# Four of six modulation chunks of layer 0 summed as rows on VectorE instead of on TensorE, no row sums in the first MLP tiles, two order tables replaced

## The chip, the cores and the metric

The kernel runs on one core of a Trainium2 chip. A core has TensorE (PE, matrix products, with its weight loads shown as PEld), VectorE (DVE), ScalarE (ACT), GpSimd (POOL) and SyncE (SP, which issues most DMA transfers). Each engine takes its own instructions in program order; semaphores hold an instruction until what it needs is there. The metric is the device time of one execution in microseconds (us).

## The reference

Two layers work on 512 latent tokens of width 1024 with 256 context tokens beside them. Each layer is modulated by six vectors that come from one conditioning vector, and each has an MLP:

```
mod_l = split(silu(c) @ ada_w[i] + ada_b[i], 6)              # six chunks of 1024 per layer
a = rmsnorm(h, norm1_g[i]) * (1 + mod_l[1]) + mod_l[0]
# layer 0: differential attention (4 heads) || Hyena-2 channels, one input, one output projection
# layer 1: multi-scale pooling mixer
h = h + mod_l[2] * y
h = h + mod_l[5] * (relu((rmsnorm(h, norm2_g[i]) * (1 + mod_l[4]) + mod_l[3]) @ w1[i]) ** 2 @ w2[i])
```

Layer 0 uses chunks 0 and 1 for the context tokens too. Chunk 2 is wanted at the end of layer 0's mixing, chunks 3 and 4 at its MLP's norm, chunk 5 behind the MLP. The output is the final RMS norm of h.

## The kernel before

Matrices of fp32 are split into a high part of 12 bits and a low rest, and a product is three passes: high by high, high by low, low by high. So each weight tile of 128x1024 is loaded by SP into a ring of four buffers (`sraw`), its high part is made on ACT (`whi`) and its low part on POOL or DVE (`wlo`).

The first third (start and mixing of layer 0) follows two tables, `START` and `MIDDLE`: each word is a step and its number, as `u12`, and a last `v` or `g` puts its elementwise work on DVE or POOL. `play` runs the steps in the order of the table, and that is the order on every engine. The steps that matter here:

- `lg`, `gv`, `ga`, `gt`, `gm`: load chunks 1 and 0 of layer 0 from `adaN`, multiply them with silu(c) and silu(c_ctx) on PE (accumulator `gav`, four products side by side with 32 columns of weights each), copy the sums out and transpose them to columns (`gat`), finish the vectors.
- `lr`, `rv`, `ra`, `rt`, `rm`: the same for chunks 2 to 5 by silu(c): 32 loads of 128x1024 into `sraw`, 16 products steps on PE (accumulator `rav`), then copy, transpose, finish.
- `sb`, `sc`: silu(c) spread over all partitions as a row (`sbcl`).
- `hw`: small products that only keep PE at work. `kp`, `ny`: the spectrum of the Hyena filter (`kp`, `kn`).
- `x`, `w`, `r`: load, high part and low part of an input weight tile. `u`: four products of an input projection. `vm`, `va`, `vh`, `vl`: the attention values, product, bias on DVE (which frees one of two accumulators), high and low part. `S`, `M`, `E`, `C`: attention scores, row maxima on DVE, exponentials on ACT, combination.

Behind the tables comes layer 0's output projection and then Python loops: an MLP of four blocks; a block has eight tiles `f` (first matrix, with `f_out`: relu and square on ACT, square again and low part on DVE) and eight tiles `r` (second matrix, `h_add` on DVE); block 0 does its first four `f` in halves, and block 3 ends with the norm of what follows. Layer 1's modulation is summed in these loops by `grow`: each call multiplies a loaded 128x1024 piece of the transposed `ada_w` with `sbcl` on DVE and sums its rows (one `tensor_tensor_reduce`, shown as CUSTOM_DVE_ANT_0 and a read of the accumulator), 48 in all. In block 0 it is called twice a tile `f`, elsewhere once a tile.

```
        for b in range(4):
            pe.matmul(dst[32 * b : 32 * b + 32, :], sil2[:, 2 * k : 2 * k + 32],
                      srcs[b // 2][:, b % 2 * T : (b % 2 + 1) * T], ...)   # gemv_tile, L571
```

Of the kernel before, what the change touches and what calls it, by code (L numbers as in the profile page):

```python
# [12 lines left out]
ALU = mybir.AluOpType  # L13
# [80 lines left out]
def body(ctx: ExitStack, tc: tile.TileContext, I, out):  # L94
# [517 lines left out]
    rav = {}  # L612
# [15 lines left out]
    @step("rm")
    def row_mods(r):
        gr = gat[1 + r][:, 0]  # L630
        o = (2 + 2 * r) * ND
        if r == 0:
            pairs = ((mods[:, 0, 2, :], 0), (mods[:, 0, 3, :], 1))
        else:
            pairs = ((mods[:, 0, 5, :], 1),)
            dst = smul[:, 1, :]
            dve.tensor_tensor(out=by_half(dst), in0=gr[:, 0], in1=by_half(gpre[:, 1, :]), op=ALU.add)
            dve.tensor_tensor(out=dst, in0=dst, in1=pr("n2g", 0, ND), op=ALU.mult)
        for dst, c in pairs:
            dve.tensor_tensor(  # L640
                out=by_half(dst), in0=gr[:, c], in1=by_half(pr("ada_b", o + c * ND, o + (c + 1) * ND)), op=ALU.add
            )
# [1372 lines left out]
```

## Time and profile before

| what | value |
|---|---|
| median of 3 runs (lowest, highest) | 1135.11 us (1133.04, 1138.07) |
| profiled execution, its own time | 1135.81 us |
| its span, first to last instruction | 1134.0 us |
| mean granted TensorE clock | 0.992 |
| PE busy | 1106.3 us, 98% of the span |
| DVE, ACT, POOL busy | 638.0, 440.5, 396.2 us |

The three runs spread by 0.44%. A busy PE is not a PE at its peak, since its instructions overlap: two matmuls of 128x512 behind each other start about 0.23 us apart, and each is shown with about 0.39 us. So the start-to-start distances tell what a product costs. Where the profile gives an idle time in square brackets, it names what ended it.

### The profile page before, as it was taken

Reading aid. Unit: us, or ns where it says so; the run is one execution under the profiler, and the core shown is the slowest. Engines: PE = TensorE matmul, PEld = TensorE weight load, DVE = VectorE, ACT = ScalarE, POOL = GpSimd, SP = SyncE. Lnnn points to the kernel's source line nnn. Section 1 sums busy time; section 2 is a strip of 40 time slices with the busy share of each in tenths; the row PEclk is TensorE's granted clock in tenths of the full one; section 3 lists DMA queues with packets and bytes.
Section 4 is the critical chain, followed back from the end, with each engine's and each line's share of the span. In section 5 each row is a group of like instructions: output and inputs, shape, how many; then the busy total and the mean of one; then the engine's idle time right before and its main releaser. Section 6 shows DMA issues by size and latency. Waiting matters only on the chain.

```text
span 1134.0 us, 14938 instructions
## 1 busy us (share of the span) xinstructions
PE 1106.3 (98%) x5876; PEld 922.4 (81%) x5876; DVE 638.0 (56%) x964; ACT 440.5 (39%) x741; POOL 396.2 (35%) x307
## 2 busy tenths in 40 slices
PE   8999999999999999999999999999999999999996
PEld 6578787888989978888888888899888888888886
DVE  5855237988965686677677532677323322332334
ACT  3563235666743531142232133366322412412331
POOL 4453245766664511122123113355211221131212
PEclk9999999999999999999999999999999999999998
DMA  9777555113642357657567523213232231231302
GB/s 334 282 239 247 169 203 158 48 40 101 204 168 97 108 167 246 217 167 250 198 202 243 184 75 111 75 38 112 76 110 75 87 137 55 94 113 73 112 1 75
DMA packets 48651, 161.38 MB, mean 142 GB/s; under 512 B 5250, under 2 KB 8578, under 8 KB 48452
## 3 DMA queue, kind: packets, MB, share of 16 engines
q1 hardware_dynamic: 46132, 149.93, 39.1%
q0 software_dynamic: 2448, 10.49, 2.7%
q8 instruction: 46, 0.75, 0.3%
q14 instruction: 25, 0.20, 0.1%
HBM read 156.20 MB, written 4.20 MB: 141 GB/s over the span
## 4 chain that ended last, share of the span: by engine, by line
PE 85%; DVE 6%; DMA 3%; ACT 3%; issue 2%; POOL 1%; SPq 0%; POOLq 0%; ACTq 0%; DVEq 0%
PE r L201 11%; PE r L197 11%; PE r L195 11%; PE f L201 9%; PE f L197 9%; PE f L195 9%; PE v L890 3%; PE u L201 2%; PE u L195 2%; PE u L197 2%; DMA g<-in_adaN 2%; PE rav L571 1%; DVE nl L1523 1%; PE wk L408 1%; PE f L1624 1%
## 5 line engine op out<-in xcount | busy, mean ns | idle before, releaser
L164 POOL TENSOR_TENSOR wlo<-raw,whi 128x1024 fp32r<-128x1024 f32 x77 | 194.9, 2534 | 524.8 <-ACT whi L163 381.4
L197 PE MATMUL r<-gl,whi 128*128 128x512 f32 (+1 forms) x576 | 207.3, 368 | 2.1 <-DVE gl L1615 2.1
L163 ACT CAST whi<-raw 128x1024 fp32r<-128x1024 f32 x135 | 140.0, 1043 | 178.3 <-PE r L197 153.4
L195 PE MATMUL r<-gh,whi 128*128 128x512 f32 (+1 forms) x576 | 207.6, 369 | 0.0
L195 PE MATMUL f<-nh,whi 128*128 128x512 f32 (+1 forms) x512 | 191.4, 379 | 0.0
L197 PE MATMUL f<-nl,whi 128*128 128x512 f32 (+1 forms) x512 | 191.3, 378 | 0.0
L1536 DVE SCALAR_TENSOR_TENSOR h<-r,mods,h 128x512 f32<-128x512 f32 (+1 forms) x81 | 54.3, 671 | 170.6 <-PE r L201 170.4
L1614 DVE TENSOR_TENSOR r<-r 128x512 f32<-128x512 f32 (+1 forms) x72 | 53.9, 749 | 165.4 <-ACT gh L1613 165.2
L1612 ACT ACTIVATE r<-f 128x512 f32<-128x512 f32 (+1 forms) x72 | 39.6, 550 | 236.5 <-PE f L201 234.9
L201 PE MATMUL r<-gh,wlo 128*128 128x512 f32 (+1 forms) x576 | 131.4, 371 | 0.0
L197 PEld LDWEIGHTS r<-gl,whi 128*128 128x128 f32 x576 | 108.5, 188 | 21.6 <-DVE gl L1615 2.5
L195 PEld LDWEIGHTS r<-gh,whi 128*128 128x128 f32 x576 | 108.6, 189 | 19.3
L201 PE MATMUL f<-nh,wlo 128*128 128x512 f32 (+1 forms) x512 | 121.3, 379 | 0.0
L201 PEld LDWEIGHTS r<-gh,wlo 128*128 128x128 f32 x576 | 101.2, 190 | 19.1
L195 PEld LDWEIGHTS f<-nh,whi 128*128 128x128 f32 x512 | 96.2, 188 | 19.0
L197 PEld LDWEIGHTS f<-nl,whi 128*128 128x128 f32 x512 | 96.3, 188 | 18.9
L201 PEld LDWEIGHTS f<-nh,wlo 128*128 128x128 f32 x512 | 92.3, 188 | 18.9
L1465 DVE CUSTOM_DVE_ANT_0 g<-g,sbcl 128x1024 f32<-128x1024 f32 x48 | 98.6, 2054 | 0.4 <-DMA g<-in_adaT 0.4
L164 DVE TENSOR_TENSOR wlo<-raw,whi 128x1024 fp32r<-128x1024 f32 x58 | 76.4, 1317 | 8.4 <-ACT whi L163 8.4
L195 PE MATMUL u<-ah,whi 128*128 128x512 f32 x160 | 63.3, 396 | 0.0
L197 PE MATMUL u<-al,whi 128*128 128x512 f32 x160 | 62.6, 391 | 0.0
L1485 ACT ACTIVATE sq<-h 128x256 f32<-128x256 f32 (+1 forms) x47 | 21.4, 460 | 80.4 <-DVE h L1536 80.4
(373 smaller groups left out, 1847.2 us busy)
## 6 DMA issues: line engine op xcount, KB each, us to landing
raw<-in_w SPq DMA_DIRECT2D x128, 512.0 KB, 4.5
g<-in_adaN SPq DMA_DIRECT2D x48, 512.0 KB, 5.6
g<-in_adaT SPq DMA_DIRECT2D x48, 512.0 KB, 3.5
raw<-in_w_hy SPq DMA_DIRECT2D x12, 512.0 KB, 3.9
raw<-in_w_qk SPq DMA_DIRECT2D x8, 512.0 KB, 5.2
pth<-in_pth POOLq DMA_DIRECT2D x4, 768.0 KB, 6.3
raw<-in_w_out SPq DMA_DIRECT2D x5, 512.0 KB, 4.0
x<-in_xT SPq DMA_DIRECT2D x8, 256.0 KB, 5.2
```

What stands on the lines that cost most here:

```text
L163: act.copy(out=hi, in_=src)
L164: (lo_eng or dve).tensor_tensor(out=lo, in0=src, in1=f32(hi), op=ALU.subtract)
L195: pe.matmul(ps, wh[:, c], ah[i][:, t0 : t0 + n], start=(i == 0), stop=False)
L197: pe.matmul(ps, wh[:, c], al[i][:, t0 : t0 + n], start=False, stop=False)
L201: pe.matmul(ps, wl[:, i * P : (i + 1) * P], ah[i][:, t0 : t0 + n], start=False, stop=(i == k - 1))
L408: pe.matmul(t[:, 0:P], idn, idn, start=True, stop=True)
L890: pe.matmul(pp[:, :256], a, b, start=(k == 0 and e == 0), stop=(k == ND - 1 and e == 2))
L1465: dve.tensor_tensor_reduce(out=gin[k], in0=gin[k], in1=sbc[0], scale=1.0, scalar=0.0, op0=ALU.mult, op1=ALU.add, accum_out=mods[:, layer, ...
L1485: act.activation(out=sq, in_=hs[d][:, seg], func=AF.Square)
L1536: dve.scalar_tensor_tensor(out=hs[d][:, seg], in0=pp[:, :n], scalar=gate[:, d : d + 1], in1=hs[d][:, seg], op0=ALU.mult, op1=ALU.add)
L1612: act.activation(out=r, in_=pp[:, :n], func=AF.Relu)
L1614: dve.tensor_tensor(out=r, in0=r, in1=r, op=ALU.mult)
```

## The change

1. Chunks 2 to 5 of layer 0 come from the transposed `ada_w` (which now holds both layers) and are summed as `grow` does it: 32 steps `rv`, each one `tensor_tensor_reduce` on DVE. The 16 product steps, two copies on ACT and eight transposes on PE go; `rm` is now four steps of one or two small additions on DVE. `sb` and `sc` stand ahead of the first `rv`.
2. `grow` is no longer called in block 0's tiles `f`; since 48 sums are wanted, the last eight now fall in block 3's tiles `f`.
3. Both tables hold another order, and other engines for some elementwise steps.

```diff
 START = """
-ws0v lx7 lx0 lx6 hw7 fm0 hw15 lx1 hw11 kc0 wh0 ft0 al0 hw5 gp0 fs0 lx3 sq3 fm1 wl0v ws1v ld0 sq7 hw13 hw0 lx5 lc2 lx2
+ws1v lx0 lg4 hw11 fm0 hw13 ft0 hw22 lx2 hw0 fs0 sq2 gp0 fm1 ws0v hw4 hw23 hw2 hw5 wh1 gp3 ft1 wh0 lx4 lx1 sq1 fs1 wl1v
...
@@ row_load
-        nc.sync.dma_start(out=rows_in[k], in_=I["adaN"][k % 16 // 2, :, 2 + 2 * (k // 16) + k % 2, :])
+        nc.sync.dma_start(out=rows_in[k], in_=I["adaT"][0, (2 * ND + k) * P : (2 * ND + k + 1) * P, :])
@@ row, row_out, row_t, row_mods
-    @step("rv")
-    def row(n):
-        r, k = n // ND, n % ND
-        acc_ = lazy(rav, 0, lambda: ps_sc("rav"))[:, r * T : (r + 1) * T]
-        gemv_tile(acc_, k, (rows_in[2 * n], rows_in[2 * n + 1]))
-
-    @step("ra")
-    def row_out(r):
-        gemv_copy(1 + r, rav[0][:, r * T : (r + 1) * T])
-
-    @step("rt")
-    def row_t(r):
-        gemv_columns(1 + r)
...
+    @step("rv")
+    def row(k):
+        g = rows_in[k]
+        dve.tensor_tensor_reduce(
+            out=g, in0=g, in1=sbc[0], scale=1.0, scalar=0.0, op0=ALU.mult, op1=ALU.add,
+            accum_out=mods[:, 0, 2 + k // ND, k % ND : k % ND + 1],
+        )
+
+    @step("rm")
+    def row_mods(i):
+        c = 2 + i
+        m = mods[:, 0, c, :]
+        if c == 4:
+            dve.tensor_tensor(out=smul[:, 1, :], in0=m, in1=gpre[:, 1, :], op=ALU.add)
+            dve.tensor_tensor(out=smul[:, 1, :], in0=smul[:, 1, :], in1=pr("n2g", 0, ND), op=ALU.mult)
+        else:
+            dve.tensor_tensor(out=m, in0=m, in1=pr("ada_b", c * ND, (c + 1) * ND), op=ALU.add)
@@ mlp
-                grow(2 if blk == 0 else 1)
+                if blk:
+                    grow()
@@ _pack
-    x["adaT"] = asc(g["ada_w"][1:].transpose(0, 2, 1))
+    x["adaT"] = asc(g["ada_w"].transpose(0, 2, 1))
-    x["adaN"] = asc(a0[:, :, [1, 0, 2, 3, 4, 5], :])
+    x["adaN"] = asc(a0[:, :, [1, 0], :])
```

Three places show how instructions move. The first is PE at the end of the first two chunks' products (`gav`), ahead of the input projections; `kp` and `kn` are the filter's spectrum, `gat` the transposes of the sums. Before:

```order
L571 MATMUL gav_321<-g_439,sil_78 32x512 x2
L551 MATMUL kn_457<-pmh_366,altm 128x512
L552 MATMUL kn_457<-pml_388,altm 128x512
L551 MATMUL kn_457<-pmh_421,altm 128x512
L552 MATMUL kn_457<-pml_455,altm 128x512
L553 MATMUL kn_457<-midh,altr 128x512
L554 MATMUL kn_457<-midl,altr 128x512
L571 MATMUL gav_321<-g_468,sil_78 32x512 x2
L571 MATMUL gav_321<-g_472,sil_78 32x512 x2
L186 MATMUL kp_400<-pmh_429,cs_214 128x512
L187 MATMUL kp_400<-pml_470,cs_214 128x512
```

And now:

```order
L571 MATMUL gav_315<-g_396,sil_78 32x512 x2
L571 MATMUL gav_315<-g_425,sil_78 32x512 x2
L571 MATMUL gav_315<-g_416,sil_78 32x512 x2
L571 MATMUL gav_315<-g_431,sil_78 32x512 x2
L584 MATMUL gat_445<-idn,gas_443 128x128 x4
L186 MATMUL kp_453<-pmh_389,cs_325 128x512
L187 MATMUL kp_453<-pml_413,cs_325 128x512
L188 MATMUL kp_453<-pmh_389,cs_307 128x512
L186 MATMUL kp_463<-pmh_386,cs_325 128x512
L187 MATMUL kp_463<-pml_450,cs_325 128x512
L188 MATMUL kp_463<-pmh_386,cs_307 128x512
```

The six `kn` products and 12 of the `kp` products, which stood ahead of the last `gav`, stand behind it now: 52 `kp` where it was 40, and six `kn` where it was none.

The second is DVE while PE makes the attention values: `v` is the bias that frees a value accumulator, `vl`, `wv` and `wlo` are low parts, `ISA g,mods` the row sum and `ISA mods` the read of its accumulator. Before:

```order
L896 TENSOR_TENSOR v_1025<-v_985,vbias_704 128x256
L734 TENSOR_TENSOR wv_970<-raw_842,wv_968 128x512
L734 TENSOR_TENSOR wv_971<-raw_842,wv_969 128x512
L737 TENSOR_TENSOR wlo_1072<-raw_889,whi_1070 128x1024
L896 TENSOR_TENSOR v_1094<-v_1004,vbias_704 128x256
L896 TENSOR_TENSOR v_1102<-v_1043,vbias_704 128x256
L896 TENSOR_TENSOR v_1124<-v_1081,vbias_704 128x256
L907 TENSOR_TENSOR vl_700<-v_1094,vh_696 128x128
```

And now:

```order
L882 TENSOR_TENSOR v_1065<-v_1032,vbias_704 128x256
L627 ISA g_994,mods<-g_994,sbcl 128x1024
L627 ISA mods 128x1
L882 TENSOR_TENSOR v_1095<-v_1070,vbias_704 128x256
L627 ISA g_1026,mods<-g_1026,sbcl 128x1024
L627 ISA mods 128x1
L893 TENSOR_TENSOR vl_702<-v_1095,vh_698 128x128
L893 TENSOR_TENSOR vl_703<-v_1095,vh_699 128x128
L882 TENSOR_TENSOR v_1153<-v_1112,vbias_704 128x256
L627 ISA g_1067,mods<-g_1067,sbcl 128x1024
L627 ISA mods 128x1
```

Between two `v` there is now a row sum or two. Up to the first row maximum of the attention DVE has 28 row sums where it had none, and four `wlo` of 128x1024 where it had ten; the other four row sums stand among the attention's steps.

The third is DVE in block 0 of layer 0's MLP: `r` and `gl` are the square and the low part of a tile `f` of 512 columns. Before:

```order
L1614 TENSOR_TENSOR r_4323<-r_4323 128x512
L1615 TENSOR_TENSOR gl_4297<-r_4323,gh_4296 128x512
L1465 ISA g_4328,mods<-g_4328,sbcl 128x1024
L1465 ISA mods 128x1
L243 TENSOR_TENSOR mods<-mods,prm 128x1
L1465 ISA g_4330,mods<-g_4330,sbcl 128x1024
L1465 ISA mods 128x1
L243 TENSOR_TENSOR mods<-mods,prm 128x1
L1614 TENSOR_TENSOR r_4367<-r_4367 128x512
L1615 TENSOR_TENSOR gl_4341<-r_4367,gh_4340 128x512
```

And now:

```order
L1600 TENSOR_TENSOR r_4276<-r_4276 128x512
L1601 TENSOR_TENSOR gl_4250<-r_4276,gh_4249 128x512
L1600 TENSOR_TENSOR r_4310<-r_4310 128x512
L1601 TENSOR_TENSOR gl_4284<-r_4310,gh_4283 128x512
L164 TENSOR_TENSOR wlo_4318<-raw_4151,whi_4317 128x1024
L1600 TENSOR_TENSOR r_4348<-r_4348 128x512
L1601 TENSOR_TENSOR gl_4322<-r_4348,gh_4321 128x512
L1600 TENSOR_TENSOR r_4386<-r_4386 128x512
L1601 TENSOR_TENSOR gl_4360<-r_4386,gh_4359 128x512
```

The eight row sums are gone from between the tiles, and each `gl` follows its own square.

## Rows read from the trace of the kernel before

**Rows 1.** Windows: us, busy PE PEld DVE ACT POOL (x), clock, DMA share, GB/s.

```profile
45.20:68.10 22.90, 22.90 (x106) 17.74 (x104) 17.23 (x28) 18.30 (x27) 6.86 (x5) 1.00 0.67 224
68.10:183.20 115.10, 113.56 (x712) 87.92 (x711) 49.92 (x87) 44.12 (x87) 47.67 (x53) 1.00 0.60 201
183.20:333.60 150.40, 147.34 (x881) 127.38 (x880) 128.12 (x222) 90.43 (x193) 96.94 (x98) 1.00 0.36 117
...
417.30:427.30 10.00, 7.89 (x28) 5.98 (x27) 8.86 (x15) 4.18 (x5) 2.68 (x1) 0.83 0.62 224
...
96.00:150.00 54.00, 53.17 (x411) 44.49 (x408) 18.79 (x42) 15.32 (x41) 13.49 (x23) 1.00 0.59 204
...
183.00:230.00 47.00, 45.08 (x246) 37.20 (x245) 38.09 (x62) 30.45 (x61) 29.11 (x25) 1.00 0.29 89
...
425.00:714.00 289.00, 289.00 (x1275) 236.71 (x1275) 178.22 (x230) 82.84 (x104) 71.34 (x33) 1.00 0.55 186
```

**Rows 2.** Tile `rav` on PE, and two timeline rows: start us, us, what.

```profile
L571 PE MATMUL rav<-g,sil x128: 592/592/617, 68.1 to 184.6; 128*32 128x512 f32 x128
...
68.13 1.07 PE L571 MATMUL rav<-g,sil 128*32 128x512 f32 x8
69.13 0.61 PE L215 MATMUL nt<-sil,cssq 128*128 128x1 f32 x4
```

**Rows 3.** PE's waits, 54 to 340 us: total, times, longest.

```profile
PE rav L571 <- DMA g<-in_adaN: 1.5, 2, 0.8
```

**Rows 4.** PE timeline, one of the two groups of transposes of `rav`'s sums.

```profile
186.11 0.60 PE L584 MATMUL gat<-idn,gas 128*128 128x128 f32 x4
186.47 1.17 PE L201 MATMUL u<-ah,wlo 128*128 128x512 f32 x4
```

**Rows 5.** PE timeline, end of the first two chunks' products.

```profile
40.62 0.50 PE L551 MATMUL kn<-pmh,altm 128*128 128x512 f32 x1
...
42.40 1.05 PE L571 MATMUL gav<-g,sil 128*32 128x512 f32 x4
44.17 1.05 PE L571 MATMUL gav<-g,sil 128*32 128x512 f32 x4 [0.71 <-DMA g<-in_adaN]
```

**Rows 6.** PE timeline, first two `r` tiles of layer 0, then of layer 1.

```profile
417.31 0.39 PE L195 MATMUL r<-gh,whi 128*128 128x512 f32 x1
...
423.07 0.50 PE L197 MATMUL r<-gl,whi 128*128 128x512 f32 x1 [2.11 <-DVE gl L1615]
...
426.42 0.63 PE L195 MATMUL r<-gh,whi 128*128 128x512 f32 x1
...
812.30 0.39 PE L195 MATMUL r<-gh,whi 128*128 128x512 f32 x1
...
817.90 0.39 PE L195 MATMUL r<-gh,whi 128*128 128x512 f32 x1
```

**Rows 7.** Row sums of `grow`: by line (busy, mean ns), then ns min/median/max.

```profile
L1465 DVE CUSTOM_DVE_ANT_0 g<-g,sbcl 128x1024 f32<-128x1024 f32 x48 | 98.6, 2054 | 0.4 <-DMA g<-in_adaT 0.4
...
L1465 DVE CUSTOM_DVE_ANT_0 g<-g,sbcl x48: 1212/1223/3432, 403.6 to 643.0; 128x1024 f32<-128x1024 f32 x48
L1465 DVE DVE_READ_ACCUMULATOR2_ANT mods<- x48: 76/81/85, 404.8 to 644.2; 128x1 f32 x48
```

**Rows 8.** DVE and POOL timeline, two stretched DVE instructions and POOL's beside them.

```profile
414.69 3.42 DVE L1465 CUSTOM_DVE_ANT_0 g<-g,sbcl 128x1024 f32<-128x1024 f32 x1
...
420.29 2.73 DVE L1615 TENSOR_TENSOR gl<-r,gh 128x512 fp32r<-128x512 f32 x1
...
414.34 2.69 POOL L164 TENSOR_TENSOR wlo<-raw,whi 128x1024 fp32r<-128x1024 f32 x1 [18.99 <-ACT whi L163]
419.79 2.68 POOL L164 TENSOR_TENSOR wlo<-raw,whi 128x1024 fp32r<-128x1024 f32 x1 [2.76 <-ACT whi L163]
```

**Rows 9.** DVE by line, 68.1 to 183.2 us: busy us, mean ns, idle before.

```profile
L737 DVE TENSOR_TENSOR wlo<-raw,whi 128x1024 fp32r<-128x1024 f32 x8 | 10.3, 1292 | 12.2 <-ACT whi L728 11.8 <-ACT qh L1011 0.5
```

**Rows 10.** DMA issues, the page's part 6: KB each, us to landing.

```profile
g<-in_adaN SPq DMA_DIRECT2D x48, 512.0 KB, 5.6
```

More of the change, by code (lines that the diff above doesn't have):

```diff
@@ new lines @@
+fh0 hw21 kc0 hw16 sq0 aq1g lx7 aq2g ld0 wl0v fl0 lx5 al0 hw17 tp1 dc1 hw3 dz1 sq7 tp0 dc0 de0 lx3 sq3 hw9 hw14 lg0 gp2
+sq4 lx6 aq3 dh0 dl0 aq4g dz0 ld1 sq5 tp2 dc2 sq6 aq5g aq6g lg2 fo2v lc1 fh_2 lg1 lg3 gv0 fo4v fo5v lg5 lc0 gv1 hw15
+lg7 fh_5 gv2 hw1 fo0v lg6 hw19 gv3 aq7v hw7 hw18 tp3 lg8 hw20 lc2 lc3 lg9 lg10 ns0 fh_0 fo1v fh_1 fo3v lg11 nr0 np0
+lg12 gv4 gv5 dc3 hw10 fo6v fl_1v fo7g lg14 fl_5g nb0 lg13 nc0 fh_4 lg15 gv6 xn1v xn2v gv7 ga0 gt0 fl_0g xn5v kp2 xn4g
+fh_6 gm0 kp1 fl_4v xm5v kp3 kp7 kp0 fh_7 xm2g hw8 xm4g xh4 kp6 xm1 xh5 sb1 xl4v xh2 xn0g xn7v xm7v x1 kp5 x0 w1 xl2v
@@ new lines @@
+va6 l2 vm36 vm37 vm16 vm17 l5 rv14 vh6 vl6 lr10 f6g x10 lr16 vm18 vm19 va4 vh0 vh4 vl0g rv13 f0 vm38 vm8 rv10 vm39 va9
+l3 lr19 vm9 vm10 vm11 lr15 rv17 vh9 vl9v vm28 va2 vm29 lr12 vm30 vm31 vh3 lr20 vh1 vl1g vm20 f1v vm21 vm32 va7 vl4v
+vm22 vm23 f4g rv19 vh7 lr18 vm33 vl7v nw0 lr22 vm34 vm35 va5 lr21 rv16 w10 va8 u60 vh2 vl2v vm44 vh5 vl5v rv15 rv12
+vm45 x13 vm46 vm47 va11 vh11 u61 u62 vl3 rv20 rv18 u63 rv22 le0 r10g u64 u65 ka0 vm40 vm41 vm42 vm43 w13 r13g kx0 kx1
+x11 u78 u79 w11 u80 vl11v u66 kb0 km0v kd0 u81 va10 lr26 rv21 rv26 lr23 u82 vh8 vl8v vh10 r11v u83 u67 u68 x12 ky0 kh0
@@ new lines @@
+kl0 rm1 lr25 kx2 u69 q0 rv23 w12 kx3 s0 t0v rv25 ky1 a0v rm2 lr27 b1 lr29 u70 vl10v u71 u72 ka1 x14 u73 u74 c1v w14
+ln0 rv29 kb1 km1v b0 u75 kx4 r12g kx5 c0g S0 S2 u76 u77 kd1 lr24 u84 u85 ky2 x16 u86 kh1 r14v ka2 rv27 M2 u87 u88 x15
+E2 kb2 km2v u89 w15 kd2v u90 lr28 r15v ka3 u91 u92 kl1g u93 kh2 w16 kb3 u94 u95 S3 km3v u96 u97 kl2g M0 q1 E0 x18 rv24
+M3 kx6 rv28 S1 M1 E1 lr31 Q0 rv31 x17 Q1 r16g kx7 ky3 u98 E3 u99 S7 S6 C0 T0 M7 M6 u100 s1 kd3g u101 w18 u108 S5 x20
+u109 C1 u110 H0 L0 x19 u111 E7 kh3 M5 T1 r18 t1g a1g u112 u113 w19 u114 j16 k16 r19g u115 lr30 w17 u116 u102 E6 b2 p1
@@ new lines @@
+F2 b6 O3 M19 H8 L8 M22 N1 R1 P2 r22 p0 S23 M23 E19 C9 G0 E23 c6 f7g W1 B1 D1 E22 Q11 F0 U2 P0 K0g l21 v2 S24 G1 y2 o2
+U3 p3 v3 y3 S20 i0 u135 C11 K1g u136 M20 F1 P1 M24 A0 E20 Q10 u137 T9 i1 H9 L9 p2 S25 E24 z2 F3 j22 P3 S21 M21 E21 V4
+Q12 u138 u139 S28 O4 M25 C10 E25 T10 H10 A2v Y2 u140 M28 u141 L10 u142 u143 E28 A3 Y3 Z3g T11 S26 C12 k22 m2 A1 H11 o0
+Y0 S30 Z0g L11 V5 T12 j23 M26 E26 O5 S27 M30 F6 k23 H12 L12 E30 l19 N2 M27 E27 Q9 z3 F4 n2 Q14 I16 P6 C13 Z2g S29 Q13
+P4 I17 F7 i3 i2 I24 M29 R2 W2 T13 E29 P7 A7g A6g H13 L13 S31 M31 F5 P5 V6 B2 Y7 Y1 I8 I0 I1 E31 A5v Y5 I25 A4g m0 I9
@@ L73 @@
+Z7v Z5v I18 C14 D2 I2 O6 I26 I27 I10 I11 o1 m1 T14 I3 Z1v I12 H14 Y4 I4 Z4g C15 I5 I19 I20 Q15 I21 L14 T15 Y6 G2 I13
+Z6g I28 H15 I29 I30 n1 L15 V7 l22 I14 I6 K2g O7 I7 n0v I22 I15 d1 X1 I23 l23 e1v N3 R3 d0 g1 X10 X16 X18 W3 h1g d2 e0g
+g0 e2 X0 B3 X8 I31 g2 X9 h2g X21 X17 X13 h0 D3 G3 K3v X2 d3 X4 e3v X5 X3 g3 X12 X11 h3g X19 X20
 """.split()
@@ L610, in first_mods @@
         dve.tensor_tensor(out=by_half(dst_m), in0=gr[:, 1], in1=by_half(pr("ada_b", 0, ND)), op=ALU.add)
-    rav = {}
-    @step("rv")
-    def row(n):
-        r, k = n // ND, n % ND
-        acc_ = lazy(rav, 0, lambda: ps_sc("rav"))[:, r * T : (r + 1) * T]
-        gemv_tile(acc_, k, (rows_in[2 * n], rows_in[2 * n + 1]))
-    @step("ra")
-    def row_out(r):
-        gemv_copy(1 + r, rav[0][:, r * T : (r + 1) * T])
-    @step("rt")
-    def row_t(r):
-        gemv_columns(1 + r)
[L628 to L642, printed above, removed]
     sbc = [gm.tile([P, D], F32, name="sbcl", tag="sbc", bufs=1)]
@@ L1447, in g_fetch @@
             layer, c, j = gq[k]
-            nc.sync.dma_start(out=g, in_=I["adaT"][layer - 1, c * D + j * P : c * D + (j + 1) * P, :])
+            nc.sync.dma_start(out=g, in_=I["adaT"][layer, c * D + j * P : c * D + (j + 1) * P, :])
             gin.append(g)
```

49 lines of the change are left out of this document (13 added, 36 removed).

## The prediction, made before the changed kernel ran

> **What bounds the kernel now.** I read the windows first, to see which engine leaves no room in each stage [rows 1]. From 45.2 us, when the first two chunks are summed, to 333.6 us, the end of the mixing, PE is busy 22.90 of 22.90, 113.56 of 115.10 and 147.34 of 150.40 us; nothing else is near it in the first 115 us (DVE 49.9, POOL 47.7), while in the attention DVE comes to 128.1 of 150.4, a share of 0.85. From 425 to 714 us PE is busy all of 289.00. So PE work taken out of these stages is time won, if DVE can carry what it is given. The rows of PE's own waits come next: in the mixing PE stands 1.5 us for the row loads [rows 3]. Last I looked at the one visible hole of the MLP: in layer 0's first `r` tile PE waits 2.11 us for a low part from DVE, and the granted clock of that 10 us stretch is 0.83, that is, part of it ran at 1.2 GHz [rows 6, 1]; layer 1's same tile has no such hole [rows 6].
>
> **The change part by part.** *PE loses the 16 steps of `rav`.* One step's eight records begin at 68.13 and the next work at 69.13, so 1.00 us a step [rows 2]; 128 records are 16 steps, 16.0 us. With them go the waits for their loads, 1.5 us [rows 3], and two groups of four transposes, 186.11 to 186.47 or 0.36 us each, 0.7 us [rows 4]. All lie on the path, since PE is the full engine there: 18.2 us. The two ACT copies are off the path and cost nothing.
>
> *PE gets work behind the last `gav` that stood ahead of it.* Twelve `kp` products at 0.233 us (24 products of the same shape in the 5.60 us from 812.30 to 817.90 [rows 6]) are 2.8 us; the six `kn` took 40.62 to 42.40, 1.8 us [rows 5]. Before, they lay in time in which PE waited for loads of `adaN` (the last product began behind 0.71 us of idle for its load [rows 5]); now they stand where PE was full, 45.2 to 68.1. The loads ahead of the last `gav` are the same 30, so I let it end when it did. Cost 4.6 us; between nothing, if it ends earlier or projections are then late anyway, and a little more, since two more `hw` stand there too, uncounted.
>
> *Layer 0's first `r` tile.* It runs from 417.31 to 426.42, 9.11 us; layer 1's, with no row sums in its block's tiles, takes 5.60, 812.30 to 817.90 [rows 6]. Gain 3.5 us, most of the slow clock's part in it. With the row sums gone `gl` is ready as in layer 1, so nothing is late behind it. The eight sums and their loads go to block 3; blocks 1 and 2 carry one a tile with PE at 289.00 of 289.00 [rows 1], so they cost nothing there, and layer 1's vectors of that last chunk are wanted at the end of layer 1's first MLP block. Were that cover gone, each would be 1.3 us on DVE.
>
> *DVE gets 32 row sums.* One costs 1.22 us by the median plus 0.08 us for the accumulator, 1.30; but the mean is 2.05, 2.13 with the read [rows 7]. The difference is POOL: a sum that began at 414.69 took 3.42 us while POOL worked from 414.34 to 417.03, and a `gl` begun at 420.29 took 2.73 while POOL worked from 419.79 to 422.47 [rows 8]. So 32 sums are 41.6 us (alone) to 68.2 us (as in the MLP). I take the lower, because by the order 14 of them stand where PE makes the attention values, and there POOL is busy only 13.49 of 54.00 us [rows 1]. Up to the first row maximum the order has 28 of them, and six of the `wlo` of 1.29 us [rows 9] have gone to POOL or behind it: 49.9 - 7.8 + 28 x 1.30 = 78.5 us of DVE, its smaller exchanges taken as even.
>
> *What DVE must fit into.* PE's stage of 115.1 us loses 15 steps (15.0), the waits (1.5), one transpose group (0.4) and 36 products `u` that the order puts behind the first scores (36 x 0.233 = 8.4): 89.8 us. DVE's share goes from 0.43 to 0.87. The attention stage gets those 8.4 us of PE and four sums (128.1 + 5.2 = 133.3 us of DVE) and loses a step and a group, 157.4 us, DVE share 0.85 as before. So the first stage is now as tight as the second was: PE lost 3.06 of 150.4 us there, 2.0% [rows 1], which makes 1.8 us in 89.8. For the attention, into which four sums and their loads now reach, I take the rate of its first stretch, 1.92 of 47.0 us or 4.1% [rows 1], 6.4 instead of 3.1 us: 3.4 more. Together 5.2 us. Bounds: none, if the row sums, which nobody waits for until the end of the mixing, only fill holes; and what the rivals below take.
>
> *What is queued behind a waiting row sum.* On DVE the value biases `v`, which free PE's two accumulators, and the low parts. A row sum waits for its load, and loads share the four buffers of `sraw` with the weights; landing takes 5.6 us [rows 10]. Their number (32) and size are the same, only each buffer is now freed by DVE's sum and not by PE. The `rm` steps are small and late.
>
> *Sum.* -18.2 + 4.6 - 3.5 + 5.2 = -11.9 us. The profiled execution took 1135.8 us (1134.0 of it the span, 1.8 around it), 0.7 above the median of 1135.1; I set the difference against the median: 1123.2, say 1123.
>
> **The rivals.** *B, nothing is given back.* The filter products are hidden, because the last load lands earlier or the projections wait for their inputs in any case, and DVE's sums fill holes only: -18.2 - 3.5 = -21.7, 1113 us. For it: even the last product of `gav` waits for its load [rows 5], and what follows it needs norms and low parts from ACT, DVE and POOL first. Against it: 22.90 of 22.90 behind the last `gav` [rows 1].
>
> *C, DVE holds PE in the first stage.* In-order waiting for loads and POOL keeps DVE from more than a share of 0.77, a tenth below what the attention shows: 78.5 / 0.77 = 101.9 us instead of 89.8, 12.1 more in place of 1.8. Then -11.9 + 10.3 = -1.6, 1134 us. For it: a bias `v` stands behind one or two sums in the order, and PE has only two accumulators. Against it: DVE ran at 0.85 over 150 us with PE at 98%.
>
> *D, POOL and DVE exclude each other (slower).* Each row sum costs the MLP's 2.13 us in the stage up to the first scores: 49.9 - 7.8 + 28 x 2.13 = 101.7 us; at a share of 0.90, 113.0 us, 23.2 more than 89.8 in place of 1.8. -11.9 + 21.4 = +9.5, 1145 us. It decides from 1.82 us a sum: (42.1 + 28 x 1.82) / 0.90 = 103.4, which is 11.9 beyond 91.6. For it: the two pairs of [rows 8], and POOL busy 47.7 us of this stage. Against it: from 96 to 150 us, where half of the sums go, POOL is busy only 13.5 of 54 us [rows 1].
>
> The Trainium skill speaks for D: SBUF — State Buffer, section Who interferes with whom, says that a Vector instruction with two SBUF inputs, which a row sum is, contends with a GpSimd instruction that reads SBUF, and that the loser blocks for the whole instruction. By that rule the sums' price here would go with POOL's share; the trace agrees in the MLP ([rows 8]: the sum ended about one median after POOL did), and shows no row sum in the mixing.
>
> **How the numbers follow.** A has 0.56, B 0.18, C 0.15, D 0.11. A difference under 0.5% (5.7 us: 1129.4 to 1140.8) can't be told from none here. A's own range is 1117 to 1129 and B lies below it, so faster has 0.74; C is no change, 0.15; D is slower, 0.11. The range 1110 to 1137 takes in A, B and C with most of their spread and leaves out D and the edges.
>
> **What would show it.** On PE no `rav`, and the window up to the first scores near 90 us: then the term of 18.2 holds. The first two projections done some 4.6 us later than 68.1: the filter's term. Row sums with a median of 1.22 and a mean under 1.7 in the mixing: my price; near 2.05, D. PE's waits for `v` and `wlo` in that stage under 2 us: the first stage fits; above 10, C. Layer 0's first `r` tile at 5.60 us and a clock of 1.00 in it: the MLP's term. I am wrong if PE idles for a value's bias or a `wlo` in the mixing, or if rows' loads come late and DVE stands.

## The result, and the profile after

The changed kernel took 1121.5 us (median of four runs, 1119.41 to 1125.11) against 1134.8 us (four runs too) for the kernel before: a ratio of 0.988, with an interval of 0.985 to 0.992. The forecast was 1123, with a range of 1110 to 1137. The profiled execution took 1122.4 us, its span is 1120.6, 13.4 us shorter than that of before.

The starts of PE's work cut both spans into the same pieces (us):

| piece | before | after | difference | forecast |
|---|---|---|---|---|
| start to the end of the first two projections | 68.1 | 75.0 | +6.9 | +4.6 |
| from there to the first scores | 115.1 | 88.7 | -26.4 | -23.5 |
| to the first product `f` (367.0, 357.1) | 183.8 | 193.4 | +9.6 | +10.4 |
| to the first product `r` (417.3, 407.4) | 50.3 | 50.3 | 0 | 0 |
| to the end | 716.7 | 713.2 | -3.5 | -3.5 |
| sum | 1134.0 | 1120.6 | -13.4 | -12.0 |

(The forecast's pieces are its own terms: 89.8 + 1.8 - 115.1 in the second, 8.4 - 1.4 + 3.4 in the third.) So the sum is right within 1.5 us, though the first two rows miss by 2.3 and 2.9 us in opposite directions. These are single profiles: in that of the first experiment below, whose code up to there is the code of before, the two projections end at 66.0 us and the first scores come at 178.5, 2.1 and 4.7 us earlier. The windows of the changed kernel, with the columns of [rows 1]:

```profile
44.90:75.00 30.10, 30.08 (x130) 23.48 (x131) 21.91 (x34) 20.95 (x31) 9.74 (x6) 0.93 0.59 197
75.00:163.70 88.70, 86.36 (x551) 78.03 (x550) 82.23 (x134) 36.32 (x74) 45.38 (x42) 1.00 0.69 229
163.70:318.50 154.80, 150.42 (x888) 130.54 (x887) 142.26 (x230) 93.55 (x199) 108.19 (x105) 1.00 0.38 125
407.40:417.40 10.00, 10.00 (x45) 8.17 (x44) 4.58 (x7) 4.74 (x6) 2.70 (x1) 1.00 0.29 83
44.90:50.00 5.10, 5.08 (x16) 4.20 (x17) 2.71 (x7) 4.42 (x8) 0.00 (x0) 0.61 0.02 8
```

DVE is busy 82.23 of 88.70 us up to the first scores, a share of 0.93, and PE 0.97: two full engines beside each other. In the attention it is 0.92 and 0.97. The MLP's stretch that had 7.89 us of PE in 10 at a clock of 0.83 has 10.00 at 1.00; the first and the second `r` tile begin 5.59 us apart (before 9.11, [rows 6]):

```profile
407.36 0.39 PE L195 MATMUL r<-gh,whi 128*128 128x512 f32 x1
...
412.95 0.39 PE L195 MATMUL r<-gh,whi 128*128 128x512 f32 x1
```

The last row of the windows is new: from 44.9 us the granted clock is 0.61, so that most of this stretch ran at 1.2 GHz. PE's timeline shows what came ahead of it. Before, filter products stood there [rows 5]; now PE waits for a load:

```profile
40.55 3.69 PE L571 MATMUL gav<-g,sil 128*32 128x512 f32 x12 [4.10 <-DMA g<-in_adaN]
44.92 1.12 PE L584 MATMUL gat<-idn,gas 128*128 128x128 f32 x4 [0.69 <-ACT gas L578]
45.69 0.78 PE L186 MATMUL kp<-pmh,cs 128*128 128x512 f32 x1
...
48.82 0.43 PE L187 MATMUL kp<-pml,cs 128*128 128x512 f32 x1
49.09 0.39 PE L188 MATMUL kp<-pmh,cs 128*128 128x512 f32 x1
```

The seven products from 45.69 us on begin 0.45 us apart on the mean; from 49.09 us on it is 0.23 again. That is 1.5 us lost, and the transposes `gat` ahead of them lose 0.4 (0.77 us to the next start, 0.36 in [rows 4]). So the first row of the table comes apart like this: from the last `gav` to the end of the two projections PE takes 30.8 us (44.2 to 75.0) where it took 22.9 (45.2 to 68.1). Of the 7.9 us the 18 filter products are 4.6, two more `hw` 0.7, the wait for the sums' copy 0.7 and the slow clock 1.9; and the last `gav` ends 1.0 us earlier than before.

The row sums, first all 32 (ns: min, median, max), then the 27 between 68.1 and 163.7 us (busy us, mean ns), and one of them beside POOL's instruction of that time (DVE's timeline, then POOL's):

```profile
L627 DVE CUSTOM_DVE_ANT_0 g<-g,sbcl x32: 1208/1220/3177, 68.6 to 195.5; 128x1024 f32<-128x1024 f32 x32
...
L627 DVE CUSTOM_DVE_ANT_0 g<-g,sbcl 128x1024 f32<-128x1024 f32 x27 | 38.9, 1454 | 1.4 <-DMA g<-in_adaT 0.9 <-issue 0.5
...
87.38 3.18 DVE L627 CUSTOM_DVE_ANT_0 g<-g,sbcl 128x1024 f32<-128x1024 f32 x1
...
87.08 2.40 POOL L723 TENSOR_TENSOR wlo<-raw,whi 128x1024 fp32r<-128x1024 f32 x1
```

The mean is 1.45 us, nearer to the 1.22 of a sum alone than to the 2.05 of the MLP [rows 7]. The stretched one ends 1.08 us behind POOL's `wlo`, close to one median, as the pairs in [rows 8] do: the exclusion of POOL and DVE is there, for some of the 27.

Last, the chain of work that the first scores waited for, from 66 to 129 us (start, us, what; the longest pieces):

```profile
65.83 4.03 DMA g<-in_adaT
...
75.22 1.13 DVE g L627
...
87.46 3.10 DVE g L627
...
100.22 1.68 DVE g L627
101.91 0.35 DVE v L882
102.30 24.13 PE v L876 x198
```

It begins at a row sum's load and has only DVE's instructions and the gaps between them until 102 us, while PE has its projections to do and is not on the chain. There PE waits for the bias (PE's timeline):

```profile
102.30 0.39 PE L876 MATMUL v<-whi,ah 128*128 128x256 f32 x1 [1.58 <-DVE v L882]
```

That is the picture which the prediction's sum did not have: it added a cost on PE (the filter) to a cost on DVE (the sums) in a place where the two engines run beside each other.

### The profile page after: what moved, and what is told of

It is laid out like the page before. It is cut to its first block, busy times and chain, and to the rows that moved or that the text cites. A ratio compares the mean times of both kernels' runs of the same rounds, so it can differ in the third digit from the quotient of the medians.

```text
span 1120.6 us, 14729 instructions
## 1 busy us (share of the span) xinstructions
PE 1087.8 (97%) x5740; PEld 918.4 (82%) x5740; DVE 691.4 (62%) x1026; ACT 439.2 (39%) x740; POOL 412.4 (37%) x308
## 4 chain that ended last, share of the span: by engine, by line
PE 80%; DVE 11%; ACT 2%; DMA 2%; issue 2%; POOL 2%; SPq 0%; POOLq 0%; DVEq 0%; ACTq 0%
PE r L195 11%; PE r L197 11%; PE r L201 11%; PE f L201 10%; PE f L197 10%; PE f L195 10%; PE v L876 2%; DVE g L627 2%; PE u L195 1%; DVE nl L1509 1%; PE u L201 1%; PE u L197 1%; DMA g<-in_adaN 1%; PE f L1610 1%; DVE mx L1053 1%
## 5 line engine op out<-in xcount | busy, mean ns | idle before, releaser
L164 POOL TENSOR_TENSOR wlo<-raw,whi 128x1024 fp32r<-128x1024 f32 x77 | 194.6, 2531 | 518.1 <-ACT whi L163 384.7
L1451 DVE CUSTOM_DVE_ANT_0 g<-g,sbcl 128x1024 f32<-128x1024 f32 x48 | 105.2, 2191 | 0.0
L723 POOL TENSOR_TENSOR wlo<-raw,whi 128x1024 fp32r<-128x1024 f32 x17 | 42.5, 2499 | 37.3 <-ACT whi L714 35.5
```

The source lines that it names most:

```text
L164: (lo_eng or dve).tensor_tensor(out=lo, in0=src, in1=f32(hi), op=ALU.subtract)
L723: ew(pool if k else dve).tensor_tensor(out=wts[k][1], in0=raws[k], in1=f32(wts[k][0]), op=ALU.subtract)
L1451: dve.tensor_tensor_reduce(out=gin[k], in0=gin[k], in1=sbc[0], scale=1.0, scalar=0.0, op0=ALU.mult, op1=ALU.add, accum_out=mods[:, layer, ...
```

## The experiments

Ratios are to the kernel before, with their intervals; the changed kernel has 0.988 (0.985 to 0.992).

**No sums in the MLP's first tiles, alone.**

```diff
-                grow(2 if blk == 0 else 1)
+                if blk:
+                    grow()
```

> The kernel before with one edit: no row sums in the f tiles of layer 0's first MLP block. Theory (the prediction's term): layer 0's first r tile takes 5.6 us instead of 9.11 with no PE idle in it and the clock at 1.00, all later work comes 3.5 us earlier, and the span falls by 3.5 us to about 1130.5 (time 1131.3, ratio 0.997). Rival: the eight sums cost the same where they now are (block 3's f tiles), so PE's waits come back there and the span falls by less than 1 us.

1129.7 us, 0.9953 (0.9937 to 0.9969). The tile's distance is 5.59 us, as in the changed kernel; the gain is 4.7 us by the medians, and its interval, 3.5 to 7.1, just takes in the term of 3.5.

```profile
410.86 0.39 PE L195 MATMUL r<-gh,whi 128*128 128x512 f32 x1
...
416.45 0.39 PE L195 MATMUL r<-gh,whi 128*128 128x512 f32 x1
```

In this one profile the code ahead of the MLP, which is unchanged, also ran 6.4 us earlier than in the profile of before (loads at the start, waits for row loads). So a single pair of traces tells places, and the medians tell sums.

**The kernel before without `rav`'s products.**

```diff
-        gemv_tile(acc_, k, (rows_in[2 * n], rows_in[2 * n + 1]))
+        if k in (0, ND - 1):
+            gemv_tile(acc_, k, (rows_in[2 * n], rows_in[2 * n + 1]))
```

> The kernel before with 14 of the 16 steps of rav's products left out (first and last stay; chunks 2 to 5 are then not computed in full). Theory (the prediction's term): 14 x 1.00 us and the 1.5 us of waits for loads, -15.5 us: time 1119.3. Rival 1: a step costs more than its own 1.00 us, because the products ahead of it and behind it also start some 0.1 us later each at the change of tile size (115.72 to 115.93 and 117.78 to 118.0 where 0.115 is usual): 14 x 1.2 + 1.5 = -18.3 us, 1116.5. Rival 2: the inputs of what follows are late, and PE waits for DVE's value biases and low parts: -10 us or less, above 1124.

The edit leaves four steps of 16 standing (the first and last of each pair of chunks), not two as the expectation says, so its numbers become 12 x 1.00 + 1.5 = 13.5 us for the theory and 12 x 1.2 + 1.5 = 15.9 for rival 1. Measured: 1122.6 us, 0.9897 (0.9869 to 0.9925), -11.7 us by the ratio, with an interval from -8.5 to -14.9. In the trace the stage up to the first scores is 12.8 us shorter (102.30 for 115.10):

```profile
67.50:169.80 102.30, 99.60 (x615) 85.81 (x615) 49.09 (x84) 41.81 (x83) 47.81 (x53) 1.00 0.68 228
```

PE's busy time there falls from 113.56 to 99.60 us, 13.96 for 12 steps or 1.16 each, near rival 1's 1.2: the neighbours of a step start later too. Its idle time rises from 1.54 to 2.70 us, since it now waits for other engines (1.3 us for a copy on ACT, the rest for high parts and DVE) and not for rows. So rival 1 has the price of a step and rival 2 the waits behind it, and together they come out near the theory's sum.

**The filter ahead of the last `gav` again, by moving four `kp` steps.**

```diff
-... lg15 gv6 xn1v xn2v gv7 ga0 gt0 fl_0g xn5v kp2 xn4g fh_6 gm0 kp1 fl_4v xm5v kp3 kp7 kp0 ...
+... lg15 kp2 kp3 kp7 kp6 gv6 xn1v xn2v gv7 ga0 gt0 fl_0g xn5v xn4g fh_6 gm0 kp1 fl_4v xm5v kp0 ...
```

> The changed kernel with four filter steps (12 kp products) moved ahead of the seventh gav step again; no other edit. Theory: in the changed kernel PE waits 4.1 us for adaN's last loads and works at a granted clock of 0.50 to 0.61 from 40 to 50 us; with 2.8 us of work in that wait, the wait is 1.3 us or less and the clock stays at 1.00, so the first two projections end some 4.8 us earlier (75.2 to about 70.4 us) and the time is about 1116.7. Rival 1: only the 2.8 us are won and the clock falls as before: 1118.7. Rival 2: what follows waits for its inputs (x's low parts, weights), and nothing is won: 1121.5.

1123.0 us, 0.989 (0.987 to 0.991): nothing won. The products' own cosine tiles land as late as `gav`'s rows, so PE waits for those, and the clock falls as before (granted 0.58 from 40 to 45 us, in the changed kernel 0.50):

```profile
39.84 0.77 PE L186 MATMUL kp<-pmh,cs 128*128 128x512 f32 x1 [4.04 <-DMA cs<-in_cs]
...
44.91 0.50 PE L188 MATMUL kp<-pmh,cs 128*128 128x512 f32 x1 [1.31 <-DMA cs<-in_cs]
```

**The row sums in the order of the kernel before.** Both tables of before, in which each `rv n` becomes `rv 2n`, `rv 2n+1`:

```diff
-rv1 x3 j0 ca4g rv0 cs0 lv0 k0 ...   (the changed kernel's second table)
+x3 ca4g lr2 rv0 rv1 cs0 w2 lv0 ...  (that of before)
```

> The changed kernel with the order of the kernel before: its two tables, each rv step replaced by its two row sums in the same place, no ra and rt. Theory (DVE's sums fill holes, the order matters only at the filter): the filter products stay ahead of the last gav, so the 4.6 us (7 with the clock) are not paid, and PE waits a little more for DVE: 1135 - 18.2 - 3.5 + 5 = about 1118, range 1114 to 1122. Rival (the new order is what makes room on DVE): DVE's share of the stage up to the first scores comes to (49.9 + 41.6) / 98 = 0.93 with the sums in pairs between value biases, PE waits over 10 us for v and wlo, and the time is 1126 or more.

1149.5 us, 1.0122 (1.0098 to 1.0146): 28 us above the changed kernel and 15 above that of before, with the same steps (some 50 elementwise ones are on DVE where the changed kernel has them on POOL, or the other way; that was not tried apart). The expectation of 1118 fell. The rival was right that the order makes the room, but not in how: DVE's share of the stage is not 0.93 but 0.64 (78.47 of 122.00; the rival took 91.5, in a stage that no waits make longer), a sum's mean is 1.41 us, and still PE idles 20 us and the granted clock is 0.96.

```profile
67.20:189.20 122.00, 102.01 (x588) 88.75 (x587) 78.47 (x134) 41.44 (x82) 52.45 (x52) 0.96 0.54 180
```

DVE's timeline at PE's longest wait there, then PE's:

```profile
103.43 1.25 DVE L629 CUSTOM_DVE_ANT_0 g<-g,sbcl 128x1024 f32<-128x1024 f32 x1 [1.19 <-DMA g<-in_adaT]
...
104.62 1.75 DVE L629 CUSTOM_DVE_ANT_0 g<-g,sbcl 128x1024 f32<-128x1024 f32 x1
...
106.30 1.28 DVE L722 TENSOR_TENSOR wv<-raw,wv 128x512 fp32r<-128x512 f32 x2
108.65 1.23 DVE L725 TENSOR_TENSOR wlo<-raw,whi 128x1024 fp32r<-128x1024 f32 x1 [1.07 <-ACT whi L716]
109.79 0.75 DVE L884 TENSOR_TENSOR v<-v,vbias 128x256 f32<-128x256 f32 x2
...
110.36 0.77 PE L878 MATMUL v<-whi,ac 128*128 128x256 f32 x2 [4.95 <-DVE v L884]
```

A sum waits for its load, the next one is stretched (1.75 us), a low part waits for its high part, and the value biases `v` stand behind them all. PE had nothing to multiply from 105.4 to 110.4 us. The longest wait for a high part, 3.3 us, comes another way (the chain there): a row of sums ends, then a weight tile is loaded, split, and multiplied.

```profile
127.41 1.13 DVE g L629
128.57 4.13 DMA raw<-in_w_qk
132.81 1.05 ACT whi L716
133.91 0.79 PE u L197
```

The weights share `sraw` with the rows, so a late sum also keeps a buffer. In this stage PE waits 6.1 us for high parts, 5.9 for biases and 4.3 for a copy on ACT.

**The changed kernel with thin sums.**

```diff
-            out=g, in0=g, in1=sbc[0], ...
+            out=g[:, 0:8], in0=g[:, 0:8], in1=sbc[0][:, 0:8], ...
```

> The changed kernel with each of the 32 row sums cut to 8 of 1024 columns (loads and steps stay; chunks 2 to 5 are then not computed). DVE has some 35 us less to do up to the first scores. Theory (the prediction's term, corrected by the trace): the sums nearly only fill holes, PE's waits for v and the value biases (2.3 us from 68.1 to 163.7 us) go, and the time falls by 1 to 3 us, to about 1119.5. Rival 1 (the term as it was forecast): 5 us are given back by DVE, 1116. Rival 2 (DVE at a share of 0.93 holds PE's inputs all over, shown as longer work and not as waits): 8 us or more, 1113 or less.

1116.4 us, 0.9853 (0.9832 to 0.9873), 5.1 us below the changed kernel by the medians (3.4 by the ratios, whose intervals overlap). In the traces the first scores come 1.7 us earlier and the first `f` 5.4 us earlier: 1.7 and 3.7, where the prediction had 1.8 and 3.4. So the term of 5.2 (rival 1) fits in its places, and in its size by the medians. The expectation (1 to 3 us) was too low, for it looked at PE's waits up to the first scores alone.

**Small products in the wait.** In `gv6`, between its halves:

```diff
+            if b == 2:
+                for _ in range(16):
+                    wake(0)
```

> The changed kernel with 32 small products of 128x128 (the kernel's own steps that keep PE at work) between the two halves of the seventh gav step, where PE waits 4.1 us for a load. Theory: the clock is lost by that wait (granted clock 0.50 from 40 to 45 us, 0.61 from 45 to 50 us); with PE at work it stays at 1.00, the 15 kp products behind gav start 0.233 us apart instead of 0.43, and all that follows is some 2 us earlier (first projection's first product at 62 instead of 64.0 us; time 1119.5). Rival 1: the fall comes from the longer stretch of light work from 31 us on, and the clock falls as before: 1121.5. Rival 2: the products take longer than the wait and delay gav: 1122.5 or more.

1128.6 us, 0.9952 (0.9935 to 0.9969): slower, by a size misjudged. The fillers took 12.3 us, three times the wait of 4.1. They do show the clock's part: with PE at work the granted clock is 1.00 from 30 to 58 us, and the products behind the wait start 0.23 us apart at once.

```profile
39.96 12.26 PE L408 MATMUL wk<-idn 128*128 128x128 f32 x64
...
55.48 0.40 PE L187 MATMUL kp<-pml,cs 128*128 128x512 f32 x1
55.72 0.40 PE L188 MATMUL kp<-pmh,cs 128*128 128x512 f32 x1
```

**The first table of before, the second of the changed kernel.**

```diff
 START = """
-ws1v lx0 lg4 hw11 ...     (the changed kernel's)
+ws0v lx7 lx0 lx6 hw7 ...  (that of the kernel before)
```

> The changed kernel with the first table of the kernel before and the second table of the changed kernel (the same set of steps in each). Theory (the filter's term stands apart from the rest): 12 kp and six kn products lie ahead of the last gav again, with their own loads ahead of them as before, the clock stays at 1.00, and the first two projections end at 68 instead of 75.2 us; the rest runs as in the changed kernel, so the time is 1121.5 - 7 = 1114.5. Rival 1 (the second table is made for the first: DVE and POOL have left over from the start what the new order has done): half is lost in waits for low parts and value biases before 100 us, 1118. Rival 2: all is lost, 1121 or more.

1121.2 us, 0.9888 (0.9873 to 0.9902): the same time as the changed kernel. The first two projections end at 68.1 us, 6.9 us earlier, and the first scores come at 163.8 (163.7). Rival 2. All is lost by 100 us, where PE waits for the convolutions' sums on DVE and for a high part. The window has 7.06 us of PE's idle time (2.34 in the changed kernel) and some 2 us of slow clock; then PE's waits:

```profile
68.10:163.80 95.70, 88.64 (x552) 79.07 (x551) 86.35 (x137) 38.78 (x77) 46.45 (x43) 0.98 0.64 223
...
PE u L195 <- DVE x L830: 3.0, 2, 2.2
PE u L195 <- ACT whi L714: 2.0, 1, 2.0
```

So 6.9 us of PE's time ahead of the second table are worth nothing to the changed kernel. That the filter's 4.6 are among them follows from the chain above, where PE waits at 102 us for DVE; by itself this run exchanges a whole table.

**More sums.**

```diff
+        if k % 3 == 0:
+            dve.tensor_tensor_reduce(
+                out=g, in0=g, in1=sbc[0], ..., accum_out=junk,
+            )
```

> The changed kernel with 11 of the 32 row sums done twice (the second result goes nowhere), 10 of them up to the first scores: 13 us more of DVE in a stage of 95.6 us where it is busy 88.5. Theory (holes are what is left, the price begins when they are full): 7.1 us of holes take half, the other 6 us and the in-order waits that go with a full engine come on top: the stage grows by 6 to 10 us, time 1129. Rival 1: other work on DVE that POOL stretched now waits less, and PE's slack takes it: under 3 us. Rival 2: each doubled sum holds a value bias behind it at once: 13 us or more, 1135.

1132.2 us, 0.9984 (0.9972 to 0.9996): 10.7 us for 11 more sums, 1.0 us each (they took 20.0 us on DVE). The 32 sums that are there cost 5.1 us by the run with thin ones, 0.16 us each. By these two points the changed kernel stands at a bend: what DVE has is nearly hidden, and what would be added is not. (A doubled sum also holds its load's buffer longer, which was not tried apart.) The stage up to the first scores grows by 8.1 us, as expected, the time by 3 us more than the 1129; rival 1 is out, and rival 2's 13 are not reached.

**First table of before and thin sums together.**

> The changed kernel with the first table of the kernel before (as in the run that moved the filter back) and with the row sums cut to 8 of 1024 columns (as in the run with thin sums; chunks 2 to 5 are not computed). Theory (PE and DVE are both full up to the first scores, so that either alone gains nothing there): with both relieved the 7.5 us of the earlier projections stay, the first scores come at 154.5 us (162.0 with thin sums alone, 163.8 with the first table alone), and the time is 1116.4 - 7.4 = 1109. Rival (the second table fits only its own first table: high and low parts of weights come when they came, whatever DVE does): first scores at 160 us or later, 1115 or more.

(Edits as in the two runs above.) 1113.4 us, 0.9813 (0.9789 to 0.9838). With DVE relieved the earlier projections are worth 3.0 us by the medians (the intervals overlap), with DVE full nothing. The changed kernel pays 8.1 us for both together. The first scores come at 159.9, neither 154.5 nor quite the rival's 160. Of the 5.4 us that are missing, 0.9 lie ahead of the projections, 2.2 are one more wait on DVE at 71.7 us, and the clock of 0.98 over 90.9 us makes 1.8:

```profile
PE u L195 <- DVE x L830: 2.2, 1, 2.2
...
69.00:159.90 90.90, 87.70 (x552) 79.26 (x551) 54.57 (x139) 38.62 (x77) 42.40 (x43) 0.98 0.67 235
```

**Chunk 5 summed in the output projection.** The eight `lr` and `rv` of rows 24 to 31 leave the tables; eight loads stand behind those of `hs`, and a sum behind each of eight `h`:

```diff
+    late_load(mla, "traw", 3, 3)
...
         dve.scalar_tensor_tensor(
             out=hs[d], in0=r_pre[d], scalar=g1[:, d : d + 1], in1=hs[d], op0=ALU.mult, op1=ALU.add
         )
+        late_sum()
```

> The changed kernel with the eight row sums of chunk 5 (rows 24 to 31) taken out of the tables and put into layer 0's output projection, into buffers of their own, where DVE is busy 7.8 of 20 us (320 to 340 us). Three of them stood ahead of the first scores, five among the attention's steps. Theory (the sums among the attention's steps are the ones that cost, 3.7 of the 5.1 us that thin sums gained): first scores some 1 us earlier, the attention 3 us shorter, nothing lost in the output projection: 1117.5. Rival 1: the late loads stand ahead of the weights on SP, and PE waits in the output projection for what was won: 1121. Rival 2: the norm behind the projection is late by the sums: 1125 or more.

1127.8 us, 0.9938 (0.9916 to 0.9960): slower than the changed kernel. From the first scores to the first wait of the output projection it is 159.3 us (162.9 in the changed kernel), so the sums among the attention's steps cost what the theory said. But the first scores come 1.5 us later, and the output projection loses more than all, through a mechanism of neither rival: two of the sums, 2.78 and 2.70 us long, stand ahead of the `h` that frees PE's accumulator, and the clock falls behind the wait, granted 0.56 from 329.5 to 335 us (DVE, then PE):

```profile
322.60 2.78 DVE L1389 CUSTOM_DVE_ANT_0 g<-g,sbcl 128x1024 f32<-128x1024 f32 x1
...
325.97 2.70 DVE L1389 CUSTOM_DVE_ANT_0 g<-g,sbcl 128x1024 f32<-128x1024 f32 x1
...
328.60 0.74 DVE L1401 SCALAR_TENSOR_TENSOR h<-r,mods,h 128x512 f32<-128x512 f32 x1
...
329.49 0.77 PE L197 MATMUL r<-ath,whi 128*128 128x512 f32 x1 [4.95 <-DVE h L1401]
```

**The same with the first table of before.** The places left empty are the first three sums and the five among the attention's steps:

```diff
-rv1 x3 j0 ca4g rv0 cs0 lv0 k0 ...
+x3 j0 ca4g cs0 lv0 k0 ...
```

> As the run before with chunk 5 summed in the output projection, but with the first table of the kernel before, and with the places of the first three row sums (up to 75 us) and of the five among the attention's steps left empty (the other places hold chunks 2 to 4). Theory (PE and DVE both full): DVE loses three sums (4 us) early, the projections come 7.5 us earlier, so the first scores come some 4 us earlier than in the changed kernel and the attention is 3 us shorter: 1114.5. Rival 1: only the attention's part is won: 1118. Rival 2: the output projection loses all: 1121 or more.

1121.8 us, 0.9886 (0.9866 to 0.9907), rival 2: the output projection begins 4.5 us earlier than in the changed kernel (323.1, 327.6) and takes 5.7 us more to the first `f`.

**Chunk 5 in the MLP's first block.** This too has the first table of before. The loads stand behind the output projection's weights, the sums among the `f` tiles, none behind the last one:

```diff
+                    if layer == 0 and f < 3:
+                        late_sums(1)
...
+                elif layer == 0:
+                    late_sums((2, 2, 1, 0)[f - 4])
```

> As the run with chunk 5 late and the first table of the kernel before, but the eight sums of chunk 5 stand in layer 0's first MLP block (one after each of three f tiles of the second half pass, then two, two and one after the next three f tiles, none after the last), and their loads behind the weights of the output projection. Theory (the late loads ahead of the output projection's weights took back what was won; the attention without sums is 3 to 4.5 us shorter): the output projection begins at 323 us as in that run (327.6 in the changed kernel) and runs 29.5 us again as in the changed kernel, layer 0's first r tile takes 5.6 us, since no sum stands ahead of its last low part, and the time is 1117. Rival 1: the sums in the f tiles delay low parts as in the kernel before, and 3.5 us are lost again: 1120.5. Rival 2: the loads hold up the f tiles' weights, or the second half pass waits: 1123 or more.

1114.8 us (1112.39 to 1119.02), 0.9825 (0.9800 to 0.9851): the best of the complete kernels, 6.7 us below the changed one by the medians (the intervals just touch). The output projection begins at 320.7 us and takes 29.3 (29.5), and the `r` tile 5.60:

```profile
161.60:316.60 155.00, 153.45 (x905) 133.69 (x904) 130.88 (x224) 95.41 (x203) 107.45 (x106) 1.00 0.33 108
320.70:350.00 29.30, 29.30 (x227) 28.36 (x226) 16.32 (x29) 12.58 (x24) 13.03 (x6) 1.00 0.64 237
...
398.80 0.39 PE L197 MATMUL r<-gh,whi 128*128 128x512 f32 x1
...
404.40 0.39 PE L197 MATMUL r<-gh,whi 128*128 128x512 f32 x1
```

In the attention DVE is busy 130.88 us, 11 less than in the changed kernel, and PE stands 1.55 us where it stood 4.38.

## Why the prediction was right

*The 18.2 us of PE and the 3.5 of the MLP.* The MLP's term is exact: 3.52 us in the changed kernel and in the run that made this edit alone. That PE's work was on the path is right too: without 12 of the steps alone, the time falls by 11.7 us. But a step was priced too low, from its own start to the next one. Its neighbours pay as well: 1.16 us a step without 12 of them, and 1.23 in the changed kernel, where PE's busy time up to the first scores falls by 27.2 us, of which the 36 products and a transpose group are 8.8 and 15 steps the rest. That is some 3 us of gain which the sum did not have; it is the second row of the table.

*The filter's 4.6 us.* This step failed twice. In its own place it is larger, 6.9 us: the sum left out the two `hw`, which the prediction had named, and the fall of the clock. But in the end it costs nothing while DVE is full, as the chain and the run with the first table of before show, and 3.0 us with DVE relieved. The prediction had asked what covers each edit, and answered that PE is full there; the row that said so (22.90 of 22.90) was from a kernel in which DVE did not yet have the sums. Rival B had the half of it, projections that wait for their inputs in any case.

*DVE's 5.2 us.* Right by the thin sums in its two places, and in size by the medians (5.1; by the ratios 3.4).

*The total.* The forecast had 9.8 us of cost, 4.6 and 5.2; the run without both is 8.1 us faster than the changed kernel and 21.5 below that of before, where rival B has 21.7. That this agrees is partly luck: the run still has 3.2 us of PE's idle time up to the first scores and 1.8 of slow clock, against the 3 us of gain left out. So the total came out 1.5 us from the forecast because errors on both sides stood against each other.

*The signs.* The prediction called itself wrong if PE idles for a value's bias in the mixing. It does, for 2.4 us up to the first scores, a little over the 2 us that it allowed. The row sums' median of 1.22 us and mean under 1.7, and the `r` tile's 5.60 us, came as said.

*The price of a sum.* The 1.22 us taken were low, the mean is 1.45; over 27 sums that is 6.3 us, too little for rival D. The Trainium skill (SBUF — State Buffer, Who interferes with whom) says that a Vector instruction with two SBUF inputs contends with a GpSimd instruction that reads SBUF. The trace agrees where a sum meets POOL: 3.18 us beside `wlo`.

*Rivals C and D.* Their prices came from a share of DVE's time at which PE begins to wait. The two runs say otherwise: PE was held at a share of 0.64 in the old order, and was busy 0.97 of the stage at 0.93 in the new one. C's mechanism is real and was 28 us away, in the order that the change replaced. What the prediction called a reordering to be priced by its filter products was the condition for the whole gain. It had the order's rows in view (a bias between two sums), and took them for a risk.

What stays open: the 1.5 us by which the first scores came later when three sums were taken away ahead of them (the loads' places in the ring moved too, which was not tried apart, and two profiles of unchanged code lay 4.7 us apart at that point).

## What to carry to other kernels

When work moves from a full engine to one with room, look for what stands behind each added instruction on its engine, and for the load that waits for its buffer, not only for the receiver's share: the same 32 sums cost 28 us more in one order (and division of the elementwise steps) than in another, at a lower share. Once both engines are full, costs on the two don't add; price an edit against the chain of the new kernel, and try the removal of each alone and of both. A piece that is wanted late (here chunk 5) belongs in the nearest stretch in which nothing that frees PE stands behind it.

## What the runs showed of the hardware

The price of a wait on PE can be more than the wait: after 4.10 us for a load the products started 0.43 us apart up to 48.4 us (granted clock 0.61 from 44.9 to 50 us), and after 2.19 us in the last experiment the same for 2.7 us (granted 0.55 from 71.9 to 75.2 us):

```profile
71.94 0.77 PE L197 MATMUL u<-ah,whi 128*128 128x512 f32 x1 [2.19 <-DVE x L832]
72.50 0.63 PE L199 MATMUL u<-al,whi 128*128 128x512 f32 x1
...
75.22 0.39 PE L197 MATMUL u<-ah,whi 128*128 128x512 f32 x1
```

It does not follow each time. The same wait of 2.19 us, for the same input, stands in four runs: with the first table of before and thin sums the clock fell as here (granted 0.55), with that table alone, and with that table and chunk 5 summed in the output projection, it stayed at 1.00. So the wait's length does not decide it. After 2.07 us at 206.1 us in the changed kernel the clock stayed at 1.00 as well. Small products as a filler were dear: 64 records of 128x128 took 12.26 us at a granted clock of 1.00, 0.19 us each, where a 128x512 product takes 0.23. The kernel's own groups of four take 0.09 us each (50.73 to 51.09 us in the changed kernel); why a long row of them takes twice that was not tried.
